# Splitting weight blocks earlier in a list-scheduled hybrid backbone, with changed TensorE estimates in the scheduler

## The chip, the core and the metric

The kernel runs on one core of a Trainium2 chip. The metric is the device time of one execution in microseconds (us). The engines are TensorE (PE in the profile; its weight loads are PEld), VectorE (DVE), ScalarE (ACT), GpSimd (POOL) and SyncE (SP), which issues all DMAs here. The program holds one list of instructions for each engine, with semaphores between them.

## The reference, cut to what matters

Two layers over 1024 latent tokens ("lat") and 256 context tokens ("ctx"), model width 1024. Each layer makes one wide projection and feeds four groups of it:

```python
mod = silu(c) @ w_ada[l] + b_ada[l]                # shift, scale, gate
h = rmsnorm(x, norm_g[l]) * (1 + scale) + shift    # odd layers: column-major order
p = h @ w_in[l]                                    # 1024 x 3600
# A: gated DeltaNet, both directions: conv3 + silu on q, k, v; per 64-token chunk
#    a triangular inverse, then a scan over chunks (16 lat, 4 ctx):
#    v_new = u - w @ S;  o = qg @ S + attn @ v_new;  S = S * g + kdec^T @ v_new
# B: b_gate * conv3(c_gate * x_in)
# C: glu -> depthwise conv of 31 taps -> layernorm -> silu
# D: u * (W_s LN(v) + b) on chunks of 128 tokens
y = concat(yA, yB, yC, yD) * silu(gates)
x = x + gate * (y @ w_out[l])                      # the context too, in layer 0
```

The context scan's final state starts the latent scan. The last step is an RMSNorm of x. All is float32; the large products are made of three float32r products of split operands (a high and a low part).

## The kernel before

**Split operands.** A number x is held as hi = x rounded to float32r and lo = x - hi. A product of two such operands is hi*hi + hi*lo + lo*hi, so a 128-wide block of `w_in` takes, for each of 8 slices of the contraction and each 512 tokens, three "dense" products of 128x512 (`mm3`). The activations are the tiles hh and hl. A weight block arrives by DMA in a raw tile r (pool of 2) and is split by `split` (line 814) into a tile w (pool of 2; at the start also into u tiles): ScalarE casts the high part (`CAST w<-r`), then VectorE subtracts for the low part (`TENSOR_TENSOR w<-r,w`). The third product of a block is the first that needs the low part. `dense` (line 818) walks through a list of blocks (items); its inner `pump` takes a w tile as soon as the item before the last has released one, splits the next raw block into it, and starts the next loads.

**Where the order comes from.** The program is written down once in the order in which a small thread simulation visits its parts (class Weave), without being issued. Each instruction gets a number, its place in that text plus a "boost"; a lower number goes first. `boosted` and the AHEAD constants subtract from it: 800 for the scan of group A (`scan`), 300 for its preparation (`gdn`), 600 for the three-tap convolutions of group A (`conv3` in `group_a`), 0 for the triangular inverses (`invert`) and for h. The 31-tap convolution (`group_c_conv`: 62 passes of `SCALAR_TENSOR_TENSOR u<-u,pv,u` 128x1024 over the two halves of the channels) has no boost, nor have weight splits. Then `schedule` (line 251) makes a list schedule: at each step it takes the engine that is free first, and on it the ready instruction with the lowest number, with durations from `estimate` (line 140). All instructions thus carry line 210 in the profile. On PE two more things count. The schedule keeps an estimate of how full the array is (`op.area`), from which it predicts the array's clock; and while it thinks that the clock is or may soon be low, it takes a full-array product, if one is ready, ahead of a small one. A switch of engines' data is modelled by latencies (LAT).

**Names.** mm: PSUM of dense products. sc, ax: PSUM banks of the scans, the inverses and the other small products. In a scan step of a chunk, s is the state, x, v and at are its intermediate tiles, gs the decayed state; a step's chain is products with s, VectorE x (two passes), products with x, VectorE v, products with v, VectorE s. zd and zb are the DRAM tiles of the inverses; b_1208 and u_1182 belong to the inverse of layer 1's context; cs marks products of `w_ada`, which are filler in layer 0's scan. w_525 and w_544 are blocks of group A of layer 0 (lat), u_1203 and u_1205 hold the two halves of a token-major block of layer 1, w_1266 is a gate block of layer 1.

Of the kernel before, what the change touches and what calls it, by code (L numbers as in the profile page):

```python
# [16 lines left out]
P = 128  # L17
# [26 lines left out]

AHEAD_SCAN, AHEAD_GDN, AHEAD_INV, AHEAD_CONV, AHEAD_H = 800, 300, 0, 600, 0

LOAD, ONLY, TAU = 2.5, 3, 6

WIN, DENSE, TDENSE = 4096 / 1200, 0.4, 4
# [13 lines left out]

class Op:
    __slots__ = ("area", "alts", "eng", "fn", "cost", "prio", "deps", "users", "tiles", "ready", "ready_from", "need", "finish", "start",
                 "dma")


class Engine:
# [8 lines left out]
class Program:  # L80
# [59 lines left out]
    def estimate(self, eng, method, out, ins, args, kw):  # L140
        acc = kw.get("accum_out") is not None
        n = max(self.cols(out), max([self.cols(x) for x in ins[:1]] or [0]))
        ps = any(str(x.space) == "MemoryType.PSUM" or "PSUM" in str(x.space) for x in ins)
        ptr = sum(1 for x in ins if self.cols(x) == 1) if n > 1 else 0
        if eng == "PE":
            if method == "transpose":
                return 0.218
            lhsT, rhs = ins[0], ins[1]
            n, m, k = self.cols(rhs), self.cols(lhsT), lhsT.shape[0]
            if "r" in str(rhs.dtype).split("float32")[-1]:  # L150
                return max(0.107, n / 2400.0)
            if m <= 64 or k <= 64:
                return max(0.15, 0.05 + n * 4 / 2400.0) / self.side_by_side(k, m)
            return max(0.214, n * 4 / 2400.0) if n > 16 else 0.4
        if eng == "ACT":
            return (0.051 if ps else 0.093) + n / 1200.0 + 0.093 * (ptr + acc)
        if eng == "DVE":
            if method == "reciprocal":
                return 0.07 + n * 0.00625
            if method in ("tensor_scalar", "tensor_copy") and not ps:  # L160
                return 0.069 + n / 1920.0 + 0.06 * ptr
            return 0.069 + n / 960.0 + 0.06 * ptr
        if method == "memset":
            return 0.036 + n * 0.00083
        return 0.15 + n * 0.0021
# [20 lines left out]
    def add(self, calls):  # L186
        isap = lambda x: hasattr(x, "ap") and hasattr(x, "offset")
        eng, method, f, args, kw = calls[0]
# [3 lines left out]
        outs, ins = aps(args, kw)  # L192
        op = Op()
        i = len(self.ops)
        op.prio, op.users, op.ready, op.need, op.finish = i + self.boost, [], 0.0, 0, None
        op.alts, op.dma, op.area = {}, 0.0, 0.0
        if eng == "PE":
            op.area = 1.0 if method == "transpose" else ins[0].shape[0] * min(P, max(32, self.cols(ins[0]))) / (P * P)
        if eng == "SP":
            n = args[0].size() if callable(args[0].size) else args[0].size  # L200
            run = min(x.ap[-1][1] if x.ap[-1][0] == 1 else 1 for x in (args[0], args[1]))
            op.dma = n * 4 / 360e3 * (1.0 if run >= 128 else 2.0)
        for e, m, fn, ar, k in calls:
            table = None
            if e == "ACT" and m == "activation":
                func = ar[2] if len(ar) > 2 else k.get("func")
                table = self.TABLE.get(str(func).split(".")[-1])
# [43 lines left out]
    def schedule(self):  # L251
# [15 lines left out]
        free = {e: 0.0 for e in engs}  # L267
        busy = dict(free)
        future, avail = {e: [] for e in engs}, {e: [] for e in engs}
        dma_free, table, small = 0.0, None, False  # L270

        win, warm, act, recent = 0, False, 0.0, 0.0
        lastpe = 0.0
# [28 lines left out]
        while len(order) < len(ops):  # L302
# [45 lines left out]
                cost += 1.28  # L348
                table = tb
            if e == "PE":  # L350
                if small and cost > 0.1:
                    cost += 0.087
                small = op.alts[e][1] < 0.1
                if not warm:
                    cost *= 2
                a, b = t, t + cost
                recent = recent * math.exp((lastpe - b) / TDENSE) + op.area * (1 - math.exp(-cost / TDENSE))
                lastpe = b
                while True:
                    edge = (win + 1) * WIN  # L360
                    if b < edge:
                        act += (b - max(a, win * WIN)) * op.area * (0.75 if small else 1.0)
                        break
                    if a < edge:
                        act += (edge - max(a, win * WIN)) * op.area * (0.75 if small else 1.0)
                    warm = act > (0.35 if warm else 0.645) * WIN
                    act, win = 0.0, win + 1
            op.start, op.eng, op.fn, op.cost = t, e, fn, cost
# [91 lines left out]
class Block:  # L460
# [357 lines left out]
    def dense(self, items):  # L818
# [5 lines left out]
        def pump(i):  # L824
            while True:
                s, moved = st["s"], False
                if s < min(i + 4, n) and s in raws:
                    it = items[s]
                    if self.room(it.pool)():
                        w = self.take(it.pool, [P, 2] + it.shape, F32R)  # L830
                        self.split(w[:, 0], w[:, 1], raws.pop(s))
                        self.free("r")
                        ws[s] = w
                        st["s"] += 1
                        moved = True
                q = st["l"]
                if q < min(i + 6, n) and self.room("r")() and (items[q].cond is None or items[q].cond()):
                    raws[q] = r = self.take("r", [P] + items[q].shape)
                    items[q].load(r)
                    st["l"] += 1  # L840
                    moved = True
                if not moved:
                    return
# [1283 lines left out]
```

## Time and profile before

| | |
|---|---|
| median of 3 runs | 1433.54 us (1431.26 to 1436.95) |
| profiled execution, its own time | 1430.93 us |
| span, first to last instruction | 1429.0 us |
| mean granted TensorE clock | 0.956 of full |
| PE busy / DVE busy / ACT busy | 93% / 69% / 37% of the span |

Busy times are of one profiled execution; idle time in square brackets on a row stands before that instruction, with what ended it. A small float32 product shows as two records of the profile, a float32r product as one. A matmul's shown duration overlaps the next one's; how long it holds the engine is read from the starts.

### The profile page before, as it was taken

Reading aid. Unit: us, or ns where it says so; the run is one execution under the profiler, and the core shown is the slowest. Engines: PE = TensorE matmul, PEld = TensorE weight load, DVE = VectorE, ACT = ScalarE, POOL = GpSimd, SP = SyncE. Lnnn points to the kernel's source line nnn. Section 1 sums busy time; section 2 is a strip of 40 time slices with the busy share of each in tenths; the row PEclk is TensorE's granted clock in tenths of the full one; section 3 lists DMA queues with packets and bytes.
Section 4 is the critical chain, followed back from the end, with each engine's and each line's share of the span. In section 5 each row is a group of like instructions: output and inputs, shape, how many; then the busy total and the mean of one; then the engine's idle time right before and its main releaser. Section 6 shows DMA issues by size and latency. Waiting matters only on the chain.

```text
span 1429.0 us, 27033 instructions
## 1 busy us (share of the span) xinstructions
PE 1322.4 (93%) x10992; PEld 1053.3 (74%) x10992; DVE 986.5 (69%) x2102; ACT 526.2 (37%) x892; POOL 11.9 (1%) x76
## 2 busy tenths in 40 slices
PE   6978899987999999999999999777999999999997
PEld 4867678964787666668887787765677876788886
DVE  4788869987888544563366669898488865564454
ACT  4877432253552211132244345142364222232221
POOL 1000000000000000000000000000000000000000
PEclk9988999998999999999999999897999999999999
DMA  9646424121486544563332331404047534132732
GB/s 310 179 121 188 119 52 117 34 45 44 113 208 151 153 136 141 170 204 112 106 122 100 122 95 48 110 15 96 16 105 194 127 85 113 40 90 81 250 98 57
DMA packets 308466, 166.74 MB, mean 117 GB/s; under 512 B 148255, under 2 KB 292983, under 8 KB 308343
## 3 DMA queue, kind: packets, MB, share of 16 engines
q1 hardware_dynamic: 308342, 165.03, 42.2%
q8 instruction: 86, 1.41, 0.4%
q14 instruction: 38, 0.30, 0.1%
HBM read 124.32 MB, written 35.42 MB: 112 GB/s over the span
## 4 chain that ended last, share of the span: by engine, by line
PE 66%; DVE 16%; DMA 9%; SPq 3%; ACT 3%; issue 3%; DVEq 0%; ACTq 0%
PE mm L210 47%; PE sc L210 13%; DVE u L210 9%; PE ax L210 6%; DVE b L210 3%; SPq L210 3%; DMA x<-u 3%; DVE w L210 1%; DMA r<-in_w_in 1%; ACT b L210 1%; DMA zb<-u 1%; ACT u L210 1%; DMA b<-zb 1%; DMA u<-in_ctx 1%; ACT w L210 1%
## 5 line engine op out<-in xcount | busy, mean ns | idle before, releaser
L210 PE MATMUL mm<-hh,w 128*128 128x512 f32 x1664 | 554.3, 408 | 32.4 <-DVE w L210 28.6
L210 PEld LDWEIGHTS mm<-hh,w 128*128 128x128 f32 x1664 | 314.6, 192 | 117.0 <-DVE w L210 29.9
L210 PE MATMUL mm<-hl,w 128*128 128x512 f32 x832 | 338.8, 407 | 0.0
L210 PE MATMUL mm<-u,w 128*128 128x512 f32 (+1 forms) x1320 | 263.9, 358 | 8.6 <-ACT w L210 5.6
L210 PEld LDWEIGHTS mm<-u,w 128*128 128x128 f32 x1320 | 221.5, 194 | 43.2 <-ACT w L210 5.8
L210 DVE SCALAR_TENSOR_TENSOR u<-u,pv,u 128x1024 f32<-128x1024 f32 (+1 forms) x172 | 202.1, 1182 | 8.5 <-ACT u L210 7.4
L210 PEld LDWEIGHTS mm<-hl,w 128*128 128x128 f32 x832 | 159.4, 192 | 39.5 <-issue 7.5
L210 ACT CAST w<-r 128x1024 fp32r<-128x1024 f32 x88 | 92.5, 1052 | 227.2 <-PE mm L210 170.6
L210 DVE TENSOR_TENSOR w<-r,w 128x1024 fp32r<-128x1024 f32 x88 | 107.3, 1220 | 38.4 <-ACT w L210 38.3
L210 ACT ACT_TABLE_LOAD x83 | 106.5, 1283 | 13.5 <-DMA zd<-b 7.6
L210 DVE TENSOR_TENSOR u<-u,b 128x256 f32<-128x256 f32 (+26 forms) x246 | 89.8, 377 | 26.1 <-DMA u<-in_x 16.4
L210 PE MATMUL mm<-u,u 128*128 128x256 f32 (+1 forms) x384 | 58.3, 305 | 6.9 <-DVE u L210 5.7
L210 DVE TENSOR_TENSOR b<-u 128x30 f32<-128x30 f32 (+23 forms) x180 | 56.4, 323 | 7.4 <-DMA b<-in_conf_ln_g 2.6
L210 PE MATMUL mm<-u,hh 128*128 128x272 f32 x256 | 51.2, 298 | 10.6 <-ACT u L210 7.6
L210 PEld LDWEIGHTS mm<-u,u 128*128 128x128 f32 x384 | 53.0, 206 | 10.4 <-DVE u L210 6.8
L210 ACT ACTIVATE b<-u 128x512 f32<-128x512 f32 (+1 forms) x71 | 41.9, 607 | 41.2 <-DVE u L210 30.9
L210 PEld LDWEIGHTS sc<-s,u 64*64 64x64 f32 x1168 | 41.7, 136 | 19.1 <-issue 6.8
L210 PEld LDWEIGHTS sc<-v,u 64*64 64x64 f32 x1184 | 41.2, 134 | 19.0 <-issue 6.7
L210 ACT COPY v<-sc 128x256 f32<-128x256 f32 x36 | 13.4, 372 | 109.0 <-PE sc L210 107.4
L210 PE MATMUL sc<-s,u 64*64 64x64 f32 x1168 | 50.8, 225 | 1.6 <-DVE u L210 1.6
L210 PE MATMUL sc<-v,u 64*64 64x64 f32 x1184 | 49.1, 223 | 2.7 <-DVE v L210 2.6
L210 PEld LDWEIGHTS mm<-u,hh 128*128 128x128 f32 x256 | 41.9, 196 | 11.6 <-ACT u L210 8.0
(270 smaller groups left out, 1468.6 us busy)
## 6 DMA issues: line engine op xcount, KB each, us to landing
r<-in_w_in SPq DMA_DIRECT2D x90, 512.0 KB
u<-in_w_ada SPq DMA_DIRECT2D x16, 1024.0 KB
u<-in_x SPq DMA_DIRECT2D x16, 512.0 KB
r<-ylat SPq DMA_DIRECT2D x16, 512.0 KB
zd<-b SPq DMA_DIRECT2D x60, 128.0 KB
ylat<-g SPq DMA_DIRECT2D x24, 256.0 KB
u<-in_w_out SPq DMA_DIRECT2D x12, 512.0 KB
at<-b SPq DMA_DIRECT2D x36, 128.0 KB
```

Source lines behind the costliest of these rows:

```text
L210: op.alts[e] = ((lambda fn=fn, ar=ar, k=k: fn(*ar, **k)), cost, table)
```

## The change

Four edits: `pump` lowers the number of a weight block's two split instructions by 600 (AHEAD_SPLIT); the estimate of a float32r product grows by 0.0133 us; the surcharge of 0.087 us for a large product behind a small one gives way to 0.1 us at each change of the array's tile mode (rows x columns in use, rounded to 32, 64 or 128); and a small product's area counts the tiles that run side by side. The instructions are the same in both programs but for the table loads of ScalarE (83 before, 94 now) and for copies that may run on either engine; all others change place only. Line numbers grow by 4 to 6.

```diff
-AHEAD_SCAN, AHEAD_GDN, AHEAD_INV, AHEAD_CONV, AHEAD_H = 800, 300, 0, 600, 0
+AHEAD_SCAN, AHEAD_GDN, AHEAD_INV, AHEAD_CONV, AHEAD_H, AHEAD_SPLIT = 800, 300, 0, 600, 0, 600
...
-                return max(0.107, n / 2400.0)
+                return max(0.107, n / 2400.0 + 0.0133)
...
         if eng == "PE":
-            op.area = 1.0 if method == "transpose" else ins[0].shape[0] * min(P, max(32, self.cols(ins[0]))) / (P * P)
+            side = lambda x: 32 if x <= 32 else 64 if x <= 64 else P
+            op.mode, op.area = (P, P), 1.0
+            if method != "transpose":
+                k, m = side(ins[0].shape[0]), side(self.cols(ins[0]))
+                op.mode, op.area = (k, m), k * m / (P * P) * self.side_by_side(k, m)
...
             if e == "PE":
-                if small and cost > 0.1:
-                    cost += 0.087
-                small = op.alts[e][1] < 0.1
+                if op.mode != mode:
+                    cost += 0.1
+                mode = op.mode
...
-                        act += (b - max(a, win * WIN)) * op.area * (0.75 if small else 1.0)
+                        act += (b - max(a, win * WIN)) * op.area
...
                         w = self.take(it.pool, [P, 2] + it.shape, F32R)
+                        self.nc.boost -= AHEAD_SPLIT
                         self.split(w[:, 0], w[:, 1], raws.pop(s))
+                        self.nc.boost += AHEAD_SPLIT
```

The order on the engines changes widely; three places of it follow. First VectorE in layer 0, where the low parts of w_525 and w_544 are made, before:

```order
L210 TENSOR_SCALAR u_483<-u_483,vst_484,vr_515 128x256
L210 SCALAR_TENSOR_TENSOR u_421<-u_420,pv_73_168,u_421 128x1024
L210 TENSOR_TENSOR u_483<-u_483,b_513 128x256
L210 SCALAR_TENSOR_TENSOR u_421<-u_420,pv_73_168,u_421 128x1024
L210 TENSOR_TENSOR u_483<-u_483,b_513 128x256
L210 SCALAR_TENSOR_TENSOR u_421<-u_420,pv_73_168,u_421 128x1024
L210 TENSOR_TENSOR w_525<-r_481,w_525 128x1024
L210 SCALAR_TENSOR_TENSOR u_421<-u_420,pv_73_168,u_421 128x1024
L210 TENSOR_TENSOR w_544<-r_522,w_544 128x1024
L210 SCALAR_TENSOR_TENSOR u_421<-u_420,pv_73_168,u_421 128x1024 x6
```

and now:

```order
L214 STREAM_TRANSPOSE u_505<-u_501 128x1024
L214 TENSOR_TENSOR u_483<-u_483,b_513 128x256 x4
L214 SCALAR_TENSOR_TENSOR u_421<-u_420,pv_73_168,u_421 128x1024
L214 TENSOR_SCALAR u_483<-u_483,vst_484,vr_515 128x256
L214 TENSOR_TENSOR w_525<-r_481,w_525 128x1024
L214 TENSOR_TENSOR u_483<-u_483,b_513 128x256
L214 SCALAR_TENSOR_TENSOR u_421<-u_420,pv_73_168,u_421 128x1024
L214 SCALAR_TENSOR_TENSOR u_502<-u_505,pv_73_168,u_502 128x1024
L214 TENSOR_TENSOR u_483<-u_483,b_513 128x256
L214 SCALAR_TENSOR_TENSOR u_502<-u_505,pv_73_168,u_502 128x1024
L214 SCALAR_TENSOR_TENSOR u_421<-u_420,pv_73_168,u_421 128x1024
```

w_525's low part moved from behind the 31-tap passes (u_421) and the layernorm of group D (u_483) to a place among their first; w_544's stands 23 rows behind it now and two behind it before.

Next SyncE's queue in layer 1, where the second half of the token-major block is loaded (r_1202), before:

```order
L210 DMA r_1191<-in_w_in 128x4x256
L210 DMA zd_1183<-b_1184 128x4x64 x2
L210 DMA zd_1183<-b_1189 128x4x64
L210 DMA zd_1183<-b_1193 128x4x64 x2
L210 DMA zd_1183<-b_1198 128x4x64
L210 DMA r_1202<-in_w_in 128x4x16
L210 DMA b_1234<-zd_1183 32x8x32 x4
L210 DMA u_1147<-u_1147 32x4x32 x8
L210 DMA u_1182<-zd_1183 16x32x32 x2
L210 DMA r_1202<-in_w_in 128x4x256
L210 DMA r_1204<-in_w_in 128x8x128
```

and now:

```order
L214 DMA r_1191<-in_w_in 128x4x16
L214 DMA r_1191<-in_w_in 128x4x256
L214 DMA r_1202<-in_w_in 128x4x16
L214 DMA r_1202<-in_w_in 128x4x256
L214 DMA zd_1183<-b_1184 128x4x64 x2
L214 DMA zd_1183<-b_1189 128x4x64
L214 DMA zd_1183<-b_1193 128x4x64 x2
L214 DMA r_1204<-in_w_in 128x8x128
L214 DMA zd_1183<-b_1198 128x4x64
```

Both loads of r_1202 now stand ahead of the inverse's stores (zd) and of the shuffles (u_1147) that they stood between.

Last PE in one step of layer 0's scan, before:

```order
L210 MATMUL sc_747<-x_748,u_645 64x64 x8
L210 MATMUL ax_731<-u_719,cs_101 32x256 x3
L210 MATMUL mm_787<-hh_187,w_723 128x512 x2
L210 MATMUL sc_757<-v_657_754,u_504 64x64 x3
L210 MATMUL mm_787<-hl_188,w_723 128x512
L210 MATMUL mm_787<-hh_187,w_723 128x512 x2
L210 MATMUL mm_787<-hl_188,w_723 128x512
L210 MATMUL mm_787<-hh_187,w_723 128x512 x2
L210 MATMUL mm_787<-hl_188,w_723 128x512
L210 MATMUL mm_787<-hh_187,w_723 128x512
L210 MATMUL sc_757<-v_657_754,u_504 64x64 x5
L210 MATMUL sc_753<-v_658_755,u_645 64x64 x8
L210 MATMUL ax_736<-b_732,sel_103 2x256
```

and now:

```order
L214 MATMUL sc_747<-x_748,u_645 64x64 x8
L214 MATMUL ax_731<-u_719,cs_101 32x256 x3
L214 MATMUL mm_787<-hl_188,w_723 128x512
L214 MATMUL mm_787<-hh_187,w_723 128x512
L214 MATMUL sc_757<-v_657_754,u_504 64x64 x8
L214 MATMUL sc_753<-v_658_755,u_645 64x64 x8
L214 MATMUL ax_736<-b_732,sel_103 2x256
```

The run of dense products (mm) between the scan's products is two long now and ten before. Counted so over whole stretches (dense products alone): inside layer 0's latent scan 186 before and 72 now; inside layer 1's 137 and 69; ahead of layer 0's scan 1618 and 1663; between w_1139, the first block of layer 1, and the products of the last context's inverse (ax_1248) 601 and 736; behind layer 1's scan 709 and 742. PE changes its tile mode 516 times before and 429 times now. On VectorE, w_1266's subtraction stands 79 instructions earlier than before; in the program's first part, those of the context's blocks stand up to 88 earlier, while the last low part of layer 0's h keeps its place in the list.

## Rows read from the trace of the kernel before

**Rows 1.** The page: busy time of the engines; the chain that ended last.

```profile
PE 1322.4 (93%) x10992; PEld 1053.3 (74%) x10992; DVE 986.5 (69%) x2102; ACT 526.2 (37%) x892; POOL 11.9 (1%) x76
...
PE 66%; DVE 16%; DMA 9%; SPq 3%; ACT 3%; issue 3%; DVEq 0%; ACTq 0%
```

**Rows 2.** Waits of PE: us in total, times, longest us.

```profile
PE mm L210 <- DVE w L210: 31.2, 5, 16.5
...
PE mm L210 <- ACT w L210: 8.0, 3, 5.6
```

**Rows 3.** Windows, by stage: us, busy us of each engine, granted clock, DMA share, GB/s.

```profile
0.00:160.00 160.00, 126.90 (x980) 112.37 (x980) 120.75 (x383) 106.89 (x208) 5.09 (x42) 0.88 0.66 186
...
296.50:472.00 175.50, 157.44 (x1117) 118.47 (x1115) 143.61 (x287) 71.87 (x93) 0.32 (x2) 0.91 0.48 112
472.00:626.00 154.00, 151.83 (x2142) 98.72 (x2142) 79.00 (x177) 31.54 (x64) 0.20 (x4) 1.00 0.54 161
...
837.50:987.00 149.50, 120.88 (x718) 104.58 (x717) 134.44 (x246) 51.75 (x83) 0.15 (x1) 0.89 0.31 73
...
1156.00:1257.00 101.00, 97.40 (x1708) 72.91 (x1709) 60.47 (x136) 22.65 (x45) 0.00 (x0) 0.98 0.28 73
```

**Rows 4.** Timeline, layer 0's wait: ACT, DVE, PE (start us, us, instruction, idle before).

```profile
297.17 1.05 ACT L210 CAST w<-r 128x1024 fp32r<-128x1024 f32 x1
...
328.82 1.22 DVE L210 TENSOR_TENSOR w<-r,w 128x1024 fp32r<-128x1024 f32 x1
...
330.10 1.22 PE L210 MATMUL mm<-hh,w 128*128 128x512 f32 x2 [12.06 <-DVE w L210]
```

**Rows 5.** Timeline, layer 1's long wait: ACT, DVE, PE.

```profile
945.19 1.05 ACT L210 CAST w<-r 128x1024 fp32r<-128x1024 f32 x1
...
973.18 1.21 DVE L210 TENSOR_TENSOR w<-r,w 128x1024 fp32r<-128x1024 f32 x1
...
974.44 1.22 PE L210 MATMUL mm<-hh,w 128*128 128x512 f32 x2 [16.54 <-DVE w L210]
```

**Rows 6.** Timeline, layer 1's token-major block: SP, ACT, PE.

```profile
904.86 1.17 SPq L210 DMA_DIRECT2D r<-in_w_in  x2
...
909.14 1.10 ACT L210 CAST u<-r 128x1088 fp32r<-128x1088 f32 x1 [5.43 <-DMA r<-in_w_in]
...
910.29 1.05 PE L210 MATMUL mm<-u,hh 128*128 128x272 f32 x3 [7.33 <-ACT u L210]
```

**Rows 7.** Windows right behind the two long waits.

```profile
330.10:334.80 4.70, 4.70 (x11) 3.74 (x12) 4.66 (x4) 0.00 (x0) 0.00 (x0) 0.50 0.61 170
...
974.50:979.90 5.40, 5.40 (x13) 4.25 (x14) 5.40 (x13) 0.00 (x0) 0.00 (x0) 0.50 0.58 146
```

**Rows 8.** Timeline of PE: a lone dense product in layer 0's scan; 28 in a row.

```profile
526.14 0.68 PE L210 MATMUL sc<-v,u 64*64 64x64 f32 x16
526.76 0.50 PE L210 MATMUL mm<-hh,w 128*128 128x512 f32 x1
527.19 0.68 PE L210 MATMUL sc<-v,u 64*64 64x64 f32 x16
...
699.82 6.51 PE L210 MATMUL mm<-u,w 128*128 128x512 f32 x28
```

**Rows 9.** Timeline of ACT: a table load and the next instruction.

```profile
704.25 1.28 ACT L210 ACT_TABLE_LOAD   x1
705.55 0.20 ACT L210 ACTIVATE rs<-ss 128x1 f32<-128x1 f32 x1
```

**Rows 10.** Timeline of DVE: the state's update, two steps of layer 1's scan.

```profile
1192.24 0.42 DVE L210 TENSOR_TENSOR s<-gs,sc 128x256 f32<-128x256 f32 x1 [1.87 <-PE sc L210]
...
1197.35 0.42 DVE L210 TENSOR_TENSOR s<-gs,sc 128x256 f32<-128x256 f32 x1
```

**Rows 11.** Windows in layer 1's scan.

```profile
1177.90:1188.10 10.20, 7.90 (x159) 6.30 (x159) 4.44 (x11) 2.26 (x6) 0.00 (x0) 1.00 0.47 99
1188.20:1191.50 3.30, 3.30 (x25) 2.34 (x25) 1.57 (x4) 0.37 (x1) 0.00 (x0) 0.50 0.23 84
```

More of the change, by code (lines that the diff above doesn't have):

```diff
@@ L67 @@
     __slots__ = ("area", "alts", "eng", "fn", "cost", "prio", "deps", "users", "tiles", "ready", "ready_from", "need", "finish", "start",
-                 "dma")
+                 "dma", "mode")
 class Engine:
@@ L195, in add @@
         op.prio, op.users, op.ready, op.need, op.finish = i + self.boost, [], 0.0, 0, None
-        op.alts, op.dma, op.area = {}, 0.0, 0.0
+        op.alts, op.dma, op.area, op.mode = {}, 0.0, 0.0, None
         if eng == "PE":
-            op.area = 1.0 if method == "transpose" else ins[0].shape[0] * min(P, max(32, self.cols(ins[0]))) / (P * P)
+            side = lambda x: 32 if x <= 32 else 64 if x <= 64 else P
[3 more added lines that the diff above has]
+                op.mode, op.area = (k, m), k * m / (P * P) * self.side_by_side(k, m)
         if eng == "SP":
@@ L269, in schedule @@
         future, avail = {e: [] for e in engs}, {e: [] for e in engs}
-        dma_free, table, small = 0.0, None, False
+        dma_free, table, mode = 0.0, None, None
         win, warm, act, recent = 0, False, 0.0, 0.0
@@ L361, in schedule @@
                     if b < edge:
-                        act += (b - max(a, win * WIN)) * op.area * (0.75 if small else 1.0)
+                        act += (b - max(a, win * WIN)) * op.area
                         break
                     if a < edge:
-                        act += (edge - max(a, win * WIN)) * op.area * (0.75 if small else 1.0)
+                        act += (edge - max(a, win * WIN)) * op.area
                     warm = act > (0.35 if warm else 0.645) * WIN
```

## The prediction

> **What bounds the kernel now.** I read the busy times first [rows 1]: PE works in 93% of the span and makes 66% of the chain that ended last, so the end comes earlier only if PE waits less, runs less of its work at the low clock, or has less to do. PE's idle time is 1429.0 - 1322.4 = 106.6 us. The waits of PE [rows 2] tell what ends it: the low parts of weight blocks, made by VectorE, end 31.2 us of it in only 5 waits, the longest 16.5 us; the high parts, cast by ScalarE, end 8.0 us. The table by stage [rows 3] tells where. Up to 160 us PE is idle for 33.1 us, from 296.5 to 472 (before layer 0's latent scan) for 18.1, from 837.5 to 987 (layer 1's blocks ahead of its scan) for 28.6; the two scans' stages have 2.2 and 3.6 us. In the two later poor stages the granted clock is 0.91 and 0.89, against 1.00 in layer 0's scan. VectorE is busy there in 143.6 of 175.5 us and 134.4 of 149.5 us: it is not idle while PE waits, it does something else first. That is the picture of a wrong order, not of a lack of VectorE; but VectorE has only 32 and 15 us to spare in these stages, and that limits what a better order can give.
>
> **What the change does, part by part.**
>
> *The long wait of layer 0.* ScalarE casts w_525 at 297.17, VectorE subtracts at 328.82, 31 us later, and PE waits 12.06 us for it [rows 4]. In the new order that subtraction stands among the first passes that it stood behind (first pair of order rows). The wait goes: -12.1 us. What is late next is w_544's subtraction, 23 rows behind: summed over these rows with the durations that the same instructions have in the trace, about 16 us of VectorE, while PE has one block, 48 dense products of 0.23 us, or 11 us. w_525 is ready before PE needs it, so I count no wait there, at most 5 us.
>
> *The long wait of layer 1.* The same picture: cast at 945.19, subtraction at 973.18, PE idle for 16.54 us [rows 5]. The number that moved it back was that of the inverse's and layernorm's passes; w_1266's subtraction now stands 79 instructions earlier on VectorE. -16.5 us.
>
> *The token-major block of layer 1.* PE waits 7.33 us for u_1205, whose cast waited 5.43 us for its load; SyncE issued that load at 904.86 [rows 6], behind the shuffles and the inverse's loads that stand ahead of it in its queue. In the new order both halves of it stand ahead of them (second pair of order rows), because the blocks before are split earlier and release the raw tile earlier: -7.3 us. The price is a wait that was not there: the inverse's first stores now stand behind a load that waits for the raw tile of w_1201, whose subtraction is one VectorE pass of 1.2 us among its producers. Behind these stores hangs the last context's inverse. I bound this by 0 and 3 us, and take 2.
>
> *The clock behind the waits.* Behind each of the two long waits PE works at half clock for 4.70 and 5.40 us [rows 7]. At the full clock half of that is enough: -5.0 us, if the waits go.
>
> *Fewer changes of the tile mode.* A lone dense product between scan products holds PE from 526.76 to 527.19, 0.43 us; in a row of 28 one takes 6.51 / 28 = 0.23 us [rows 8]. So an excursion costs 0.20 us. The new order has 516 - 429 = 87 changes fewer, or 43 excursions: -8.7 us, all of it PE's own work.
>
> *The start.* The ScalarE waits include one of 5.6 us in the first stage [rows 2], and splits stand up to 88 instructions earlier there. But h is finished at the same place of VectorE's list, and VectorE is busy for 120.8 of 160 us [rows 3]. Bounds 0 and -14 us (all weight waits of the stage, with the half clock behind them); I take -4, nearer to none, since VectorE sets the pace.
>
> *Table loads.* ScalarE gets 94 - 83 = 11 more. The row shows 1.28 us for one, and the next instruction starts 0.02 us later [rows 9]. That is 14.1 us on an engine that is busy for 37%; I count nothing, since splits, evacuations and scan copies have idle time around them, and 14.1 us if that cover were gone everywhere. The Trainium skill, "ScalarE: Activation LUTs", section "What ACT_TABLE_LOAD costs", speaks against this change more strongly: it adds a drain to each load, 2.66 us for a switch, so 29 us here by an estimate from that page; the row shows no such drain, and the measured 1.28 us is used.
>
> *What VectorE gives back.* The dense products that PE does early, because it no longer waits, bring it sooner to work that VectorE must finish first. The place is the last context's inverse: 736 - 601 = 135 more dense products stand ahead of it. PE's work in the stage becomes 120.9 + 135 x 0.23 = 152 us, less 3 us of lost half clock: 149 us. VectorE must do 134.4 us plus one or two splits in the same time. Both now fit about equally; I take 3 us of new waits here, with 15 us (all of VectorE's idle time there) as the upper end.
>
> *Thinner scans.* The scans lose their filler: 186 to 72 dense products in layer 0's, 137 to 69 in layer 1's. A step of layer 1's scan takes at least 1197.35 - 1192.24 = 5.11 us in the trace [rows 10]. PE's part of a step is now 40 products, of which 8 hold PE from 526.14 to 526.76 [rows 8], so 3.1 us, with some 4 dense ones, 1 us, and side products and excursions of about 0.7 us: 4.8 us. So PE falls 0.3 us per step short, for 16 steps 5 us; layer 0's scan has the w_ada products as filler and I add 1 us. Bounds 0 and 16 x 1 x 2 = 32 us.
>
> Sum: -12.1 - 16.5 - 7.3 + 2 - 5.0 - 8.7 - 4 + 3 + 6 = -42.6. From the profiled execution's 1430.9 us that leaves 1388; the median of the runs lies 2.6 us above that execution, so I forecast 1391 us.
>
> **Rivals.**
>
> *VectorE sets the starts of both scans.* If the inverses and the 31-tap passes, now behind the splits, keep PE waiting at the scans, about half of the gain is lost. For: 90% of VectorE in the stage from 837.5 [rows 3]. Against: VectorE's work ahead of layer 0's scan is the same to 2 us, and it has 32 us of idle time there. Gain: the 45 extra dense products ahead of layer 0's scan, 10.4 us, as much again in layer 1, and half of the excursions, 4.4 us: -25, so 1408 us.
>
> *Nothing net.* The change doesn't reach its aim where it matters: the scan of layer 1 ends when it did, and 742 instead of 709 dense products stand behind it, 33 x 0.23 = +7.6 us; less the excursions' 8.7 us, that is 1432 us. For: layer 1's scan is a chain of VectorE and PE in turn. Against: PE is busy for 97.4 of its 101 us [rows 3], so the chain was not what set its pace.
>
> *Slower: the scans lose the clock.* The filler kept the array full. In layer 1's scan PE was busy for 7.9 of 10.2 us, and in the next 3.3 us it worked at half clock [rows 11]. PE's work in the two scans would be 151.8 + 97.4 - 182 x 0.23 = 207 us. Each us of it at half clock costs one more, so 42 us, a fifth of it, eats the gain; a third of it, 69 us, gives 1391 + 69 = 1460 us. Against: most of both scans ran at 1.00 and 0.98 [rows 3] with small products as the larger part. The Trainium skill, "TensorE: Matmul & The Clock Gate", section "What's actually happening", says that the throttled state is the default and that activity releases it; the rows agree, and by that rule this rival has its chance wherever PE comes to wait in the scans.
>
> **How the numbers follow.** Forecast case (1370 to 1405): 0.60. Half lost (1405 to 1422): 0.22. Better than forecast, because the start and layer 0's other idle time shrink too: 0.03. Nothing net: 0.07. Slower: 0.08. A range from 1367 to 1421 leaves out the last two and a little of the first ends; the unknown terms (start -14 to 0, VectorE 0 to 15, scans 0 to 32) fit into it unless several go one way. Faster by over 0.5% (below 1426.4; 0.5% is about what a measurement tells from no change): 0.85; within 0.5%: 0.07; slower: 0.08.
>
> **What would show it.** Right: no PE wait over 5 us on a w tile between 296 and 990; the load of u_1205 issued before 895 on the old axis; layer 0's scan starting 15 us or more earlier, its steps shorter than 7 us; 95% PE busy between w_1139 and the scan. Wrong: PE waiting for the inverse (ax) or inside the scans' chain for more than 15 us together, a granted clock under 0.95 in a scan, or new weight waits elsewhere.

## The result, and the profile after

The changed kernel takes 1383.12 us (median of 4 runs, 1378.18 to 1389.51) where the kernel before takes 1433.0 (4 runs); the ratio is 0.9645, with a 95% interval of 0.9614 to 0.9677. The forecast was 1391 us.

| | before | after |
|---|---|---|
| profiled execution, us | 1430.93 | 1382.8 |
| its span, us | 1429.0 | 1381.1 |
| mean granted clock | 0.956 | 0.969 |
| PE busy, us (share) | 1322.4 (93%) | 1299.9 (94%) |
| VectorE busy, us | 986.5 | 986.2 |
| ScalarE busy, us | 526.2 | 539.9 |

All lines of the program are called L214 now. First the waits of PE in the page of the changed kernel (us in total, times, longest), which answer to [rows 2]:

```profile
PE ax L214 <- issue: 9.5, 4, 4.0
PE ax L214 <- ACT b L214: 5.8, 4, 2.4
PE sc L214 <- DVE b L214: 5.4, 2, 3.0
...
PE mm L214 <- ACT w L214: 1.2, 1, 1.2
PE mm L214 <- DVE w L214: 0.6, 1, 0.6
```

The 31.2 us for the low parts of weight blocks are 0.6 us, the 8.0 us for the high parts 1.2. At the head of the list stand the inverses (ax), with waits of 4 us at most. Now the stages between the same events of the program as in [rows 3] (start:end, length, busy us of PE, PEld, VectorE, ScalarE, GpSimd, granted clock, DMA share, GB/s):

```profile
0.00:162.60 162.60, 128.12 (x991) 113.71 (x992) 123.48 (x381) 107.64 (x211) 5.10 (x42) 0.91 0.67 192
...
299.40:464.00 164.60, 160.42 (x1129) 122.24 (x1127) 138.47 (x275) 79.31 (x98) 0.31 (x2) 0.98 0.51 124
464.00:603.00 139.00, 136.94 (x2108) 90.80 (x2108) 83.29 (x185) 35.00 (x68) 0.20 (x4) 0.99 0.67 196
...
814.10:963.00 148.90, 144.22 (x852) 124.54 (x851) 136.00 (x248) 62.43 (x96) 0.35 (x5) 0.99 0.36 86
963.00:1119.00 156.00, 147.20 (x1382) 112.94 (x1384) 128.84 (x280) 70.84 (x91) 2.42 (x8) 0.92 0.45 110
1119.00:1202.00 83.00, 74.56 (x1625) 58.36 (x1621) 54.17 (x127) 18.42 (x40) 0.00 (x0) 0.96 0.26 68
```

The two poor stages are full: ahead of layer 0's scan PE is idle for 4.2 us (18.1 before), in layer 1's blocks for 4.7 us (28.6 before). The stages behind them are now the poorer ones: from 963 to 1119 PE is idle for 8.8 us at a granted clock of 0.92, in layer 1's scan for 8.4 us (3.6 before).

The splits themselves: w_525 (cast at 299.64), w_1266 (cast at 906.42) and u_1205 (cast at 867.31), on ScalarE, VectorE and PE, which answer to [rows 4 to 6]:

```profile
299.64 1.05 ACT L214 CAST w<-r 128x1024 fp32r<-128x1024 f32 x1 [2.53 <-PE mm L214]
...
300.77 1.22 DVE L214 TENSOR_TENSOR w<-r,w 128x1024 fp32r<-128x1024 f32 x1
...
906.42 1.06 ACT L214 CAST w<-r 128x1024 fp32r<-128x1024 f32 x1 [1.18 <-PE mm L214]
...
912.11 1.21 DVE L214 TENSOR_TENSOR w<-r,w 128x1024 fp32r<-128x1024 f32 x1
...
867.31 1.11 ACT L214 CAST u<-r 128x1088 fp32r<-128x1088 f32 x1 [2.12 <-DMA r<-in_w_in]
...
871.55 0.41 PE L214 MATMUL mm<-u,hh 128*128 128x272 f32 x2
```

From cast to subtraction it is 1.1 us instead of 31.7 for w_525 and 5.7 instead of 28.0 for w_1266; PE stands at none of the three. What came instead is in layer 1, on PE:

```profile
963.01 1.20 PE L214 MATMUL ax<-b,b 32*32 32x32 f32 x64 [4.04 <-issue]
...
1104.79 1.19 PE L214 MATMUL ax<-b,b 32*32 32x32 f32 x64 [3.79 <-issue]
```

Both are first products of an inverse. At 1104.79 PE has done 2568 dense products of 128x512, as it seems all that can be done before this inverse: six kernels below (split_only, no_mode, old_area, no133, sub_only, inv300) stop at the same number. In the kernel before 2526 were done at this point (1147.17), and PE did not wait.

Where the 47.9 us of the span come from, by stages between first products of the same blocks (worked out from the records, like the next table):

| stretch, up to the first product of | before | after | difference |
|---|---|---|---|
| w_401 (start) | 161.4 | 164.0 | +2.6 |
| w_521 | 135.1 | 135.4 | +0.3 |
| w_924 (layer 0's blocks and scan) | 340.1 | 314.0 | -26.1 |
| w_1139 | 200.9 | 200.7 | -0.2 |
| u_1205 (layer 1's first blocks) | 72.8 | 57.4 | -15.4 |
| w_1541 (layer 1's other blocks and scan) | 364.9 | 355.6 | -9.3 |
| the end | 153.8 | 154.0 | +0.2 |

And by kind: idle time of PE (between its products, and behind the last one, together the prediction's 106.6 us before), half of its busy time at the low clock, and the rest, PE's own work at the full clock:

| | before | after | difference |
|---|---|---|---|
| idle between products | 96.6 | 70.9 | -25.7 |
| idle behind the last product | 10.0 | 10.2 | +0.2 |
| lost to the low clock | 42.0 | 35.3 | -6.7 |
| own work | 1280.4 | 1264.6 | -15.8 |

The two kinds of gain lie in different places. From w_521 to w_924 idle time falls by 14.0 us, the low clock's cost by 5.8 and own work by 6.5. From u_1205 to w_1541 idle time falls by 1.7 us only and the low clock costs 1.7 more: what this stretch gains is PE's own work (-9.3).

### The profile page after: what moved, and what is told of

The parts are those of the page before. It is cut to its first block, busy times and chain, and to the rows that moved or that the text cites. A ratio compares the mean times of both kernels' runs of the same rounds, so it can differ in the third digit from the quotient of the medians.

```text
span 1381.1 us, 27009 instructions
## 1 busy us (share of the span) xinstructions
PE 1299.9 (94%) x10992; PEld 1047.1 (76%) x10992; DVE 986.2 (71%) x2102; ACT 539.9 (39%) x903; POOL 11.9 (1%) x76
## 4 chain that ended last, share of the span: by engine, by line
PE 60%; DVE 15%; DMA 14%; ACT 3%; issue 3%; SPq 3%; ACTq 0%; DVEq 0%
PE mm L214 45%; PE sc L214 11%; DVE u L214 8%; DMA x<-u 6%; PE ax L214 5%; DVE b L214 3%; SPq L214 3%; DMA r<-in_w_in 3%; DVE w L214 2%; DMA u<-in_w_out 2%; ACT u L214 1%; DMA whh<-in_w_ada 1%; DMA whl<-in_w_ada 1%; DMA u<-in_x 1%; DMA b<-zb 1%
## 5 line engine op out<-in xcount | busy, mean ns | idle before, releaser
L214 PE MATMUL mm<-hh,w 128*128 128x512 f32 x1664 | 541.4, 401 | 1.7 <-ACT w L214 1.2
L214 PEld LDWEIGHTS mm<-hh,w 128*128 128x128 f32 x1664 | 311.8, 190 | 82.0 <-issue 16.5
L214 PE MATMUL mm<-hl,w 128*128 128x512 f32 x832 | 334.3, 402 | 0.0
L214 PE MATMUL mm<-u,w 128*128 128x512 f32 (+1 forms) x1320 | 261.5, 356 | 1.6 <-ACT g L214 1.1
L214 PEld LDWEIGHTS mm<-u,w 128*128 128x128 f32 x1320 | 220.0, 193 | 35.3 <-ACT g L214 1.7
L214 DVE SCALAR_TENSOR_TENSOR u<-u,pv,u 128x1024 f32<-128x1024 f32 (+1 forms) x172 | 201.9, 1182 | 1.0
L214 PEld LDWEIGHTS mm<-hl,w 128*128 128x128 f32 x832 | 157.9, 190 | 40.7 <-issue 9.3
L214 ACT CAST w<-r 128x1024 fp32r<-128x1024 f32 x88 | 92.5, 1051 | 214.4 <-PE mm L214 159.2
L214 ACT ACT_TABLE_LOAD x94 | 120.6, 1283 | 17.7 <-DMA zd<-b 5.9
L214 DVE TENSOR_TENSOR w<-r,w 128x1024 fp32r<-128x1024 f32 x88 | 107.2, 1218 | 27.3 <-ACT w L214 26.8
L214 DVE TENSOR_TENSOR u<-u,b 128x256 f32<-128x256 f32 (+25 forms) x246 | 89.3, 378 | 26.5 <-DMA u<-in_x 16.3
L214 PE MATMUL mm<-u,u 128*128 128x256 f32 (+1 forms) x384 | 56.5, 299 | 9.8 <-ACT u L214 4.2
L214 DVE TENSOR_TENSOR b<-u 128x108 f32<-128x108 f32 (+21 forms) x180 | 56.5, 323 | 7.0 <-DMA u<-zd 3.8
L214 PEld LDWEIGHTS mm<-u,u 128*128 128x128 f32 x384 | 51.2, 200 | 12.8 <-DVE u L214 5.0
L214 ACT ACTIVATE b<-u 128x512 f32<-128x512 f32 (+1 forms) x71 | 42.5, 609 | 40.4 <-DVE u L214 29.4
L214 PEld LDWEIGHTS sc<-v,u 64*64 64x64 f32 x1184 | 40.3, 138 | 16.0 <-DVE v L214 9.9
L214 PEld LDWEIGHTS sc<-s,u 64*64 64x64 f32 x1168 | 40.6, 141 | 15.1 <-DVE s L214 4.5
L214 PE MATMUL sc<-s,u 64*64 64x64 f32 x1168 | 47.3, 230 | 2.3 <-DVE u L214 1.7
L214 PE MATMUL sc<-v,u 64*64 64x64 f32 x1184 | 46.6, 226 | 2.5 <-DVE v L214 1.3
L214 PE MATMUL mm<-u,hh 128*128 128x272 f32 x256 | 48.5, 289 | 0.0
L214 ACT ACTIVATE b<-sc,mod,modG 128x128 f32<-128x128 f32 x76 | 30.9, 459 | 44.5 <-PE sc L214 26.9
L214 PE MATMUL sc<-dg,u 128*128 128x128 f32 x248 | 38.2, 311 | 8.7 <-issue 4.7
```

The source lines that it names most:

```text
L214: op.alts[e] = ((lambda fn=fn, ar=ar, k=k: fn(*ar, **k)), cost, table)
```

## The experiments

All are timed against the kernel before on the same chip. How far one profile can be trusted: the kernel of the experiment "taps" has the changed kernel's order, instruction by instruction, up to layer 1, and its profile reaches w_1139 at 820.3 us where the changed kernel's does at 814.1. Differences of some 6 us between single profiles are no finding; the sums below that carry a conclusion are larger, or are between like stages.

### Which part of the change

Theory A: the earlier splits make the gain. Theory B: the estimates make it.

The kernel before with the splits alone:

```diff
-AHEAD_SCAN, AHEAD_GDN, AHEAD_INV, AHEAD_CONV, AHEAD_H = 800, 300, 0, 600, 0
+AHEAD_SCAN, AHEAD_GDN, AHEAD_INV, AHEAD_CONV, AHEAD_H, AHEAD_SPLIT = 800, 300, 0, 600, 0, 600
+                        self.nc.boost -= AHEAD_SPLIT
                         self.split(w[:, 0], w[:, 1], raws.pop(s))
+                        self.nc.boost += AHEAD_SPLIT
```

> The kernel before with AHEAD_SPLIT = 600 alone; its estimates of TensorE are the old ones. In its order the subtractions of w_525, u_1205 and w_1266 stand 52, 26 and 98 instructions of VectorE's list earlier than before (39, 18 and 79 in the changed kernel), and PE changes between dense and other products 447 times (517 before, 429 after). Theory A, the splits that stand earlier make the gain: 1383 + 9 excursions x 0.20 = 1385 us, range 1375 to 1398. Theory B, the estimates make it (through fewer tile-mode changes and a better choice on PE): 1412 to 1433 us.

Measured: 1411.97 us, ratio 0.9861 (0.9819 to 0.9904), outside A's range and at the edge of B's. A's time is missed by 27 us. The waits on w tiles are all but gone as A says (1.9 us for casts is left), but PE now waits elsewhere: 15.8 us in one place, the last inverse before layer 1's scan, and 11.5 us in layer 0's scan (0.8 in the changed kernel).

```profile
1114.26 0.39 PE L210 MATMUL mm<-hh,w 128*128 128x512 f32 x1
1130.45 0.78 PE L210 MATMUL ax<-b,b 32*32 32x32 f32 x37 [15.80 <-issue]
```

PE's last dense product starts at 1114.26; behind it there is nothing to do until the inverse is done.

The other diffs are against the changed kernel, but for that of split_pool, which is against split_only. The estimates without the earlier splits come next. This edit sets a second constant to 0 as well, AHEAD_CONV, the boost of group A's three-tap convolutions. So the run is not the estimates alone, though what was expected calls it so:

```diff
-AHEAD_SCAN, AHEAD_GDN, AHEAD_INV, AHEAD_CONV, AHEAD_H, AHEAD_SPLIT = 800, 300, 0, 600, 0, 600
+AHEAD_SCAN, AHEAD_GDN, AHEAD_INV, AHEAD_CONV, AHEAD_H, AHEAD_SPLIT = 800, 300, 0, 0, 0, 0
```

> The changed kernel with AHEAD_SPLIT = 0: the new estimates of TensorE alone. In its order w_1266's subtraction stands where it stood before (1515 instead of 1514), u_1205's 9 and w_525's 22 instructions earlier, and there are 493 changes between dense and other products. Theory A: the wait of layer 1 stays (12 us or more on a w tile between 900 and 1000 us), at most the wait of layer 0 (12 us) goes: 1412 to 1433 us. Theory B: 1380 to 1400 us.

Measured: 1420.77 us, ratio 0.9912 (0.9879 to 0.9944), in A's range. The long wait of layer 1 (w_1266) is there, with its cause beside it: the cast at 943.71, the subtraction 21 us later.

```profile
943.71 1.05 ACT L214 CAST w<-r 128x1024 fp32r<-128x1024 f32 x1
...
964.54 1.21 DVE L214 TENSOR_TENSOR w<-r,w 128x1024 fp32r<-128x1024 f32 x1
...
965.80 1.22 PE L214 MATMUL mm<-hh,w 128*128 128x512 f32 x2 [20.06 <-DVE w L214]
```

The splits alone give 21 us, the whole change 50, so A does not hold as it stands: the splits end the waits on w tiles, and with the old estimates part of what they free ends in new waits. The 13 us of est_only belong to the estimates and the missing boost of the convolutions together. What the estimates alone are worth no run shows: layer 0's wait on w_525, which is down to 1.6 us there, may owe that to either.

Half the distance, and here too AHEAD_CONV moves along, from 600 to 300:

```diff
-AHEAD_SCAN, AHEAD_GDN, AHEAD_INV, AHEAD_CONV, AHEAD_H, AHEAD_SPLIT = 800, 300, 0, 600, 0, 600
+AHEAD_SCAN, AHEAD_GDN, AHEAD_INV, AHEAD_CONV, AHEAD_H, AHEAD_SPLIT = 800, 300, 0, 300, 0, 300
```

> The changed kernel with AHEAD_SPLIT = 300. The subtractions of w_525, u_1205 and w_1266 stand where they stood in the changed kernel to 8 instructions, that of w_1310 stands 55 later, and there are 469 changes. Theory A: the two long waits stay away, but w_1310's low part, which was 3.8 us ahead of PE, comes up to 55 x 0.47 = 26 us later, so PE waits up to 20 us for it; with 4 us for the changes 1390 to 1407 us. Theory B (order of the splits not decisive): 1383 + 4 = 1387 us and no wait on w_1310.

Measured: 1398.66 us, ratio 0.9765 (0.9718 to 0.9813), in A's range, with the wait that A names: waits for VectorE of 3.45 us on w_1280 and 8.44 us on w_1310 are back (13.2 us in 4 waits in all). How much of the 15.5 us is the splits' and how much the convolutions' was not told apart.

```profile
PE mm L214 <- DVE w L214: 13.2, 4, 8.4
```

The 600 places for the subtraction alone (inside `split`, so the subtractions of `w_out`'s blocks get them too):

```diff
     def split(self, hi, lo, raw):
         self.nc.scalar.copy(hi, raw)
+        self.nc.boost -= AHEAD_SPLIT
         self.two(lo, raw, hi.bitcast(F32), ALU.subtract)
+        self.nc.boost += AHEAD_SPLIT
```

> The changed kernel with the 600 places given to VectorE's subtraction alone and not to ScalarE's cast. The subtractions of w_525, u_1205 and w_1266 stand at 593, 1362 and 1435 in VectorE's list (585, 1362 and 1435 in the changed kernel), there are 447 changes between dense and other products and 88 table loads instead of 94. If VectorE's half of the split is what came too late: 1383 + 9 x 0.2 to 0.4 = 1385 to 1387 us, range 1380 to 1392. If the casts had to come earlier too: waits for ScalarE on w tiles, 1395 us or more.

Measured: 1387.68 us, ratio 0.9713 (0.9684 to 0.9743), in the range of the first case. It is VectorE's half that came too late. The other case's sign is there as well, but small: 6.7 us of waits for casts, the longest, of 5.1 us, in the first stage (1.2 us in all in the changed kernel). The casts' places are worth a few us at most.

```profile
PE mm L214 <- ACT w L214: 6.7, 4, 5.1
```

### Which of the estimates

```diff
-                if op.mode != mode:
-                    cost += 0.1
```

> The changed kernel with the cost of a changed tile mode (0.1 us) taken out of the planner. The splits stand within 11 instructions of where the changed kernel has them, but there are 473 changes between dense and other products instead of 429, so 22 excursions more. At 0.20 us each, as the prediction has it: 1383 + 4.4 = 1387 us, with 44 to 46 us less of PE's busy time saved than before for every such change; if a change costs nothing: 1383 us.

Measured: 1388.11 us, ratio 0.9692 (0.9652 to 0.9733), not told apart from the changed kernel's. (That each change saves 44 to 46 us of busy time, as the expectation has it, no run shows.) Own work is 3.0 us more and idle time 7.9 us, since the last inverse is waited for longer, 11.9 us; the low clock gives 2.2 us back.

```diff
-                op.mode, op.area = (k, m), k * m / (P * P) * self.side_by_side(k, m)
+                op.mode, op.area = (k, m), ins[0].shape[0] * min(P, max(32, self.cols(ins[0]))) / (P * P)
```

> The changed kernel with the old rule for a small product's area (the share of the array that the planner counts as at work, without the products beside it). Its order changes between dense and other products 525 times instead of 429; the splits stand within 7 instructions of the changed kernel's. If an excursion costs 0.20 us and that is all: 1383 + 48 x 0.20 = 1393 us (1390 to 1397). If the area is also what keeps the dense products where PE would wait without them (the 29 us by which split_only missed the changed kernel): 1403 to 1415 us. If excursions are free: 1383 us.

Measured: 1407.45 us, ratio 0.9827 (0.9782 to 0.9872), in the range of the second theory, but not by its reason: idle time and low clock are the changed kernel's (70.4 and 35.8 us), and all of the loss is own work, +21.7 us. The stage windows show it with the same products on PE. First the changed kernel, layer 0 from w_521 to w_924 and layer 1 from u_1205 to w_1541:

```profile
299.40:613.40 314.00, 307.76 (x3280) 221.37 (x3279) 228.37 (x467) 115.37 (x167) 0.52 (x6) 0.98 0.58 159
871.50:1227.10 355.60, 334.32 (x3613) 267.43 (x3612) 289.42 (x607) 135.63 (x200) 2.57 (x9) 0.95 0.39 94
```

then the kernel with the old area, the same stretches:

```profile
295.60:626.60 331.00, 320.05 (x3281) 222.52 (x3279) 228.00 (x471) 115.56 (x168) 0.52 (x6) 0.98 0.55 147
884.90:1248.80 363.90, 342.61 (x3613) 270.30 (x3612) 290.77 (x610) 134.46 (x197) 2.58 (x9) 0.96 0.38 92
```

The same number of products, at a granted clock that is the same to 0.01, holds PE for 12.3 and 8.3 us longer, with 50 and 44 changes more between dense and other products: 20.6 / 94 = 0.22 us a change, 0.44 us an excursion. The prediction had 0.20.

```diff
-                return max(0.107, n / 2400.0 + 0.0133)
+                return max(0.107, n / 2400.0)
```

> The changed kernel with a dense product estimated at n/2400 us again, 0.0133 us less. 421 changes instead of 429, the splits up to 16 instructions earlier on VectorE. If a better estimate of a dense product (0.227 us, as in the trace, instead of 0.213) is what splits need beside them: 1395 to 1412 us, with waits for the inverse as in split_only, since the planner believes PE faster than it is by 6% and places VectorE's work too late against it. If the area and the mode cost are: 1380 to 1387 us.

Measured: 1408.27 us, ratio 0.9837 (0.9791 to 0.9884), the first of the two. Own work is 2.0 us less than in the changed kernel, idle time 23.0 us more, the low clock 2.8 us. The largest wait is the same inverse again:

```profile
1118.56 0.39 PE L214 MATMUL mm<-hh,w 128*128 128x512 f32 x1
1131.24 0.99 PE L214 MATMUL ax<-b,b 32*32 32x32 f32 x53 [12.29 <-DVE u L214]
```

In this kernel 385 dense products stand between u_1205 and layer 1's context states, in the changed one 308. A planner that believes PE faster than it is uses the dense products up early, and has none when VectorE's inverse is awaited. This place makes 8.5 of the 23 us; another 8.7 are up to w_401, where a cast is waited for by 8.3 us, and 8.6 in layer 0 from w_521 to w_924; that the same reason holds there is not shown. So the three estimates do different things: the area keeps PE's changes few, the 0.0133 us keep idle time down, in layer 1 by filler for the inverse, and the mode cost does little.

```diff
-                    cost += 0.1
+                    cost += 0.3
```

> The changed kernel with 0.3 us instead of 0.1 us for a changed tile mode in the planner. 429 changes between dense and other products as before it, but 124 instead of 132 from u_1205 on, and 80 table loads instead of 94; 19 dense products, some 4.5 us of work, are still unused at the last inverse of layer 1, where the changed kernel has used all 2568 that it may use. Theory V: its wait there of 3.8 us goes, with some of the half clock behind it: 1383 - 4 - 3 = 1376 us, range 1370 to 1382. If the changed kernel's order only happens to be a good one: 1385 to 1410 us.

Measured: 1421.41 us, ratio 0.9936 (0.9918 to 0.9954). A miss: the wait for the last inverse is gone, as Theory V had it, but idle time is 25.7 us more than in the changed kernel, and 14.4 us more go to the low clock; own work (1266.5) is near that of the other kernel of 429 changes (1264.6). The idle time is spread over many places, with small loads among them:

```profile
PE sc L214 <- DMA b<-in_smlp_w: 8.8, 1, 8.8
PE sc L214 <- ACT u L214: 8.8, 5, 3.2
PE sc L214 <- DVE v L214: 7.3, 20, 0.7
```

Why a dearer mode change leads there was not settled.

### What PE waits for now

The 15.8 us of split_only stand behind a load in SyncE's queue, and the subtraction that this load waits for stands among the inverse's passes. Is the queue the cause (Theory C) or VectorE's list (D)?

```diff
+class Halves:
+    def __init__(self, real):
+        self.real = real
+    def dma_start(self, out, in_):
+        h = out.shape[1] // 2
+        self.real.dma_start(out[:, :h], in_[:, :h])
+        self.real.dma_start(out[:, h:], in_[:, h:])
...
+                    sp, self.nc.sync.real = self.nc.sync.real, Halves(self.nc.gpsimd.real)
                     items[q].load(r)
+                    self.nc.sync.real = sp
```

> The kernel of split_only (AHEAD_SPLIT = 600, old estimates), with the loads of the weight blocks' raw tiles issued from GpSimd's queue, in two halves each, instead of from SyncE's. In split_only PE waited 15.8 us for the last inverse of layer 1 (at 1130.45 us): there SyncE's queue held a raw tile's load (issued at 1118.00) that waited for a subtraction of VectorE (1116.76 to 1117.98), and the inverse's loads and stores stood behind it. Theory C, this queue is the cause: the wait falls under 6 us and most of the half clock around it (20.5 and 10.2 us in the rows of the clock) goes: 1412 - 10 - 8 = 1394 us, range 1385 to 1402. Theory D, VectorE's own list (the 31-tap passes and the inverse's passes) is the cause: the wait stays at 12 us or more, 1405 to 1416 us.

Measured: 1536.54 us, ratio 1.0719 (1.0659 to 1.0779). The time says nothing on the question, since the kernels with these loads are slow (below). The place does: no load of a raw tile stands in SyncE's queue there, and PE still waits 17.36 us. In both kernels it is 12.3 us from VectorE's last pass of this inverse to PE's first product:

```profile
1244.17 0.21 DVE L220 TENSOR_TENSOR u<-u,b 128x58 f32<-128x58 f32 x1
...
1245.30 0.34 SPq L220 DMA_DIRECT2D zb<-u  x1
1250.17 0.38 SPq L220 DMA_DIRECT2D b<-zb  x1
...
1256.71 1.19 PE L220 MATMUL ax<-b,b 32*32 32x32 f32 x64 [17.36 <-issue]
```

In split_only these two are 1118.10 and 1130.45:

```profile
1117.89 0.21 DVE L210 TENSOR_TENSOR u<-u,b 128x58 f32<-128x58 f32 x1
...
1118.00 0.39 SPq L210 DMA_DIRECT2D r<-in_w_in  x1
1118.49 2.00 SPq L210 DMA_DIRECT2D b<-zd  x4
1120.59 0.40 SPq L210 DMA_DIRECT2D zb<-u  x1
```

The queue does hold the store (zb) up there, until 2.5 us behind that pass, and only 0.9 us in split_pool, whose reload then comes later. So the queue can be some 2 us of the wait and not its main cause: C falls. A tail of a store, reloads and a transpose must be covered by dense products, and those had been used up. How far VectorE's list (D) sets the time of that last pass this run does not show.

The same edit on the changed kernel:

> The changed kernel with the same edit. Its wait for the same inverse is only 3.8 us (1104.79), its other one for an inverse 4.0 us (963.01). Theory C: the first falls to 1 to 2 us, with a little of the half clock behind it: 1377 to 1383 us. Theory D: 1383 us. If loads from GpSimd's queue land later than those from SyncE's, new waits of ScalarE on the raw tiles appear at the start and the time goes over 1387 us.

Measured: 1505.97 us, ratio 1.0509 (1.0461 to 1.0557): the third case, far beyond its bound. Nothing follows for the inverse.

```diff
-        for t in range(1, 31):
+        for t in range(1, 23 if st.l and not st.ctx else 31):
```

> The changed kernel without the last 8 of the 31 taps of layer 1's latent convolution (16 passes of 1.2 us on VectorE left out, nothing of PE's work). In its order VectorE has 235 us of work from the subtraction of w_1139 to the transpose in front of the last inverse before layer 1's scan, instead of 256. Theory V, VectorE's list is what PE now waits for in layer 1: the inverse comes up to 20 us earlier, the waits at 963 and 1104.8 us (4.0 and 3.8 us) and about half of the 23.5 us that PE works at the low clock there go: 1383 - 7.8 - 6 = 1369 us, range 1362 to 1375. Theory P, PE's own work is the bound again and its last waits are small change: 1377 to 1384 us.

Measured: 1384.59 us, ratio 0.9685 (0.9660 to 0.9709): Theory P. From w_1139 to w_1541, first the changed kernel, then this one:

```profile
814.10:1227.10 413.00, 391.07 (x3987) 316.10 (x3986) 338.11 (x685) 161.39 (x238) 2.77 (x13) 0.96 0.38 94
```

```profile
820.30:1229.20 408.90, 390.81 (x3986) 313.32 (x3985) 318.19 (x668) 155.45 (x234) 2.78 (x13) 0.97 0.39 95
```

VectorE has 19.9 us less to do and the stretch is 4.1 us shorter, no more than single profiles differ by; PE is busy for 391 us in both. The time is 0.6 us above P's range and 9.6 above V's. After the change layer 1 is bound by PE's own work again, and VectorE's list decides 4 us at most by these two profiles.

```diff
+AHEAD_SCAN, AHEAD_GDN, AHEAD_INV, AHEAD_CONV, AHEAD_H, AHEAD_SPLIT = 800, 300, 300, 600, 0, 600
```

> The changed kernel with AHEAD_INV = 300: the inverses' passes stand ahead of the 31-tap passes on VectorE where both are ready. The transpose in front of the last inverse has 2.4 us less of VectorE's work ahead of it, but there are 447 changes between dense and other products instead of 429 (9 excursions). Theory V: 1383 - 2.4 - 1.5 + 9 x 0.2 to 0.4 = 1381 to 1383 us, range 1376 to 1388; a wait for that inverse of 1 to 2 us instead of 3.8. If the passes that it delays (the convolution, and the layernorm behind it) are what PE needs next: over 1390 us.

Measured: 1393.58 us, ratio 0.9754 (0.9722 to 0.9787). Slower than V's forecast by 10 us and in the range of the second case (over 1390): the wait in front of the last inverse is 1.61 us as expected, but waits of 4.11 and 3.30 us come up in layer 0, where PE is idle for 8.5 us more from w_521 to w_924. That delayed passes of the convolution cause them was not shown. No version of these beats the changed kernel.

## Why the prediction was right, step by step

The sum was -42.6 us, the profiled executions differ by 48.1. By kind the forecast was -28.9 us of idle time (the start's 4 us among them), -5.0 of half clock and -8.7 of own work; measured were -25.7, -6.7 and -15.8. That the waits would go is right, and that is the mechanism. That the idle time comes out so near is in part luck, since its terms were off in both directions: the start gave none of its 4 us and the stretch from u_1205 to w_1541 1.7 us instead of some 5.5, but layer 0's stage 13.9 instead of 12.1 and the token-major block's stretch 10.4 instead of 7.3.

*Layer 0's wait* (-12.1): right. PE's idle time ahead of the scan fell by 13.9 us, and no wait took its place.

*Layer 1's long wait* (-16.5): it went, but not to the end of the kernel. From u_1205 to w_1541 idle time fell only from 23.0 to 21.3 us: 4.04 and 3.79 us for the inverses, 3.0 us at 1058 and 4.8 us more in the scan came in its place. The prediction had VectorE's giving back at 3 us, the stores behind a load at 2 and the scans at 6. The new waits are 15.6 us against these 11: the step was right, its share at the inverses too small. That stores behind a load in the queue are a cause split_pool bears out for some 2 us at most, in another kernel. The long wait so gave almost nothing in net idle time; what this stretch gained is own work.

*The token-major block* (-7.3): under-sized. The stretch up to u_1205 is 15.4 us shorter. Besides the wait of 7.3 us, the evacuation's wait of 2.81 us just ahead of it went, and 1.7 us of half clock; a few us are products moved behind u_1205.

*The half clock* (-5.0): -6.7 in the sum, but put together otherwise. The two stages with the long waits gave back 6.9 and 6.7 us (1.7 of them in the token-major block), the start 2.5; from 963 us, where PE first waits for an inverse, to the end of layer 1's scan 6.6 us were lost anew, and 2.9 in smaller places.

*Tile modes* (-8.7): this step was mis-sized by a factor of nearly two. The prediction priced an excursion at 0.20 us from the lone dense product of [rows 8], which shows how long PE takes to leave it. Over the twelve kernels with loads on SyncE's queue (the kernel before, the changed one and ten of the experiments), own work grows by 0.171 us (standard error 0.031) for each change between dense and other products, so by 0.34 us for an excursion; the pair with the old area gives 0.44. This is a correlation over orders, which explains three quarters of the spread. What the text ahead of the prediction calls changes of the tile mode are these changes, 517 and 429 by the count used here. With 88 fewer that is 15.1 us, and own work fell by 15.8. The Trainium skill ("TensorEngine Tiling (Array Packing)", section "Key Properties") says that a change of the tiling mode drains the engine, and gives no price; the runs agree that a change costs time. In the records the product ahead of a dense one holds PE 0.10 us longer than its like, and the dense one ahead of a small one 0.10 us (medians); together they are the prediction's 0.20, and what makes up the rest of the 0.34 us is open.

*The start* (-4): nothing came of it. w_401 begins 2.6 us later; the idle time up to it is 34.5 us (34.4 before), and the 2.5 us that the low clock gives back there are counted above.

*Table loads* (0): right. ScalarE is busy for 13.7 us more; the 11 loads more take 14.1 us (120.6 against 106.5). PE waits less for its casts than before. The page of the profile, for all 94 loads (busy, mean ns of one, idle time before):

```profile
L214 ACT ACT_TABLE_LOAD x94 | 120.6, 1283 | 17.7 <-DMA zd<-b 5.9
```

The Trainium skill ("ScalarE: Activation LUTs", section "What ACT_TABLE_LOAD costs") has 1.38 us of drain beside these 1.28. By an estimate from that page 130 us more would stand around 94 loads; the row has 17.7 us of idle time in front of them, and [rows 9] 0.02 us behind one, so that the measurement decides against it here.

*The signs.* Held: no wait on a w tile over 5 us, u_1205's load issued by 864 us (887 on the old axis), PE busy for 95.6% from w_1139 to the scan, a clock of 0.99 and 0.96 in the scans. Not held: layer 0's scan starts 8.0 us earlier and not 15, since 45 more dense products (10 us) stand ahead of it; the time appears behind the scan, where they are missing. Its steps take 7.3 us in the mean (9.5 before) where under 7 was named, 4.9 to 6.1 inside a group of four. The waits for inverses and in layer 1's scan come to 16.2 us, just over the 15 that were named as a sign against (18.3 with layer 0's scan): the waits of the rival in which VectorE sets the scans' starts are there in part, the time that it foretold (1408 us) is not, and the rival in which the scans lose the clock did not come.

What the prediction did not see is how narrow the result is. It gave the splits most of the gain and the estimates 8.7 us; with the old estimates the splits are worth 21 us of 50.

## What to carry to other kernels

Where a list schedule places the work, count a change in three sums for each stage: the bottleneck engine's idle time, its time at the low clock, and its own work. A wait that is taken away in one stage uses up the filler of the next; look there for the latency (here 12 us of store, reload and transpose behind an inverse) that the filler covered. And take each constant of the planner out by itself, with all others as they are: here the prices do not add up. Without the 0.0133 us the changed kernel loses 25 us, without the new area 24, without the mode cost 5 (not told apart from none), and without all of the new estimates at once (split_only) 29.

## What the runs showed of the hardware

Loads from GpSimd's queue, in two halves each, cost more than expected. In split_pool, where all loads of raw tiles go this way, one issue holds GpSimd for 0.75 us, and the second half of a tile mostly follows 3 to 7 us behind the first (median 3.8):

```profile
893.56 0.75 POOL L86 DMA_DIRECT2D r<-in_w_in  x1 [8.33 <-DVE ss L220]
897.30 0.76 POOL L87 DMA_DIRECT2D r<-in_w_in  x1 [3.00 <-issue]
```

The kernels with these loads take 9% longer than the same orders with SyncE's: 1536.5 against 1412.0 us, and 1506.0 against 1383.1. No run tells the queue from the halving.
